# Output projection of a hybrid attention layer: eight block products of the matrix product, or seven with sums of blocks

## The chip, the cores and the metric

The kernel runs on one core of one Trainium2 chip. The metric is device time in microseconds (us), 958.43 as the median of three runs (957.11 to 959.27).

## The reference, cut to what matters

One encoder layer over 16 meta tokens and 512 real tokens of width 2048. After the two attention mixers, the gated outputs of all 16 heads are put side by side, projected once, normalised and added to the input:

```python
ya = gqa_axial_mixer(...) * jax.nn.silu(ga)            # 8 heads of 128
yb = diff_attn_mixer(...) * jax.nn.silu(gb)            # 8 heads of 128
y = jnp.einsum('blc,cd->bld', jnp.concatenate([ya, yb], axis=-1), w_out[layer])
h = h + rmsnorm(y, post_norm_g[layer])
return h[:, N_META:, :]
```

The change concerns the `einsum` with `w_out` alone: a product of 512 x 2048 (tokens by channels) with 2048 x 2048, and what follows it.

## The kernel before, in words

Every matrix product in single precision is made of three products of a split operand: an operand `a` becomes `ah` (rounded by ScalarE, helper `hi`) and `al = a - ah` (VectorE, helper `lo`), and `mm` is issued for high x high, low x high and high x low. For weights the same split is made by `wload`: a transfer of 512 KB into a tile `st`, then `wh` on ScalarE (L150) and `wl` on VectorE (L151). The tiles `st`, `wh` and `wl` have three buffers each, in the pool `wp`. `fetch` keeps a list of chunks: it loads and splits up to three chunks ahead of the one it gives out.

Work is dealt out by a planner, `Lanes`. The dense products are the main stream; the steps of each attention head are tasks that `lanes.poll()` slips in between matmuls when a modelled clock says that they are due. The order on TensorE is thereby fixed when the kernel is built, and so is the order on every other engine, where the scheduler of the framework has put the instructions by priority. Each engine takes its instructions strictly in that order, and one that waits holds up all behind it.

All loads and stores go through the queue of SyncE (SP). GpSimd (POOL) has a few small operations of each head: the scaling of the maximum `mxA`, the scaling of the probabilities `p`, the copy `pm`, and at the end the square root `ry`.

The last dense product with the input is the gate of head A7. Up to there both kernels are the same. Then the memory of the normalised input (`xh`, `xl`, pool `xp`) is given up for the pool `op`, which holds the channels of the heads as 16 pairs `oh`, `ol` of 128 x 512. Twelve of the 16 heads come back from scratch memory in six transfers `os` of 512 KB, which use `st` buffers too; the last four heads of mixer A are taken directly from `gA`, when they are ready.

`dense_out(g)` computes 512 output columns for all four token tiles: 16 channel tiles x 4 token tiles x 3 matmuls of 128x128 by 128x512, 192 in all, and there are four of them, 768 matmuls. Each chunk of weights has two channel tiles, so it feeds 24 matmuls. During the first of the four, the last attention heads are still interleaved. Results: `collect` makes the sum of squares (ScalarE, `jko`) and multiplies by the gain (VectorE, `y`), both straight from the accumulators; `finish` does the normalisation and the residual `xr`, and stores.

Of the kernel before, what the change touches and what calls it, by code (L numbers as in the profile page):

```python
# [10 lines left out]
F32 = mybir.dt.float32  # L11
# [97 lines left out]
def kernel(ctx: ExitStack, tc: tile.TileContext, xT, xn, xm, w_s, w_t, w_q, w_o,  # L109
# [8 lines left out]
    wp = ctx.enter_context(tc.tile_pool(name="wp", bufs=3))  # L118
    dr = ctx.enter_context(tc.tile_pool(name="dr", bufs=1, space=DRAM))
# [9 lines left out]
    oscr = [dr.tile([2, P, SEQ], F32, name=f"oscr{i}", tag=f"oscr{i}") for i in range(6)]  # L129

    def ctile(shape, name, dt=F32, src=None):
        t = cst.tile(shape, dt, name=name, tag=name)
        if src is not None:
            load(t, src)
        return t
# [6 lines left out]
    def wload(src, n=1024, dma=nc.sync.dma_start, parts=1):  # L142
        st = wp.tile([P, 1024], F32, name="st", tag="st")
        wh = wp.tile([P, 1024], F32R, name="wh", tag="wh")
        wl = wp.tile([P, 1024], F32R, name="wl", tag="wl")
        for i in range(parts):
            c = slice(i * n // parts, (i + 1) * n // parts)
            dma(out=st[:, c], in_=src if parts == 1 else src[:, c])
            with tc.high_priority(AHEAD):
                nc.scalar.activation(wh[:, c], st[:, c], AF.Copy)  # L150
                nc.vector.tensor_tensor(out=wl[:, c], in0=st[:, c], in1=wh[:, c].bitcast(F32),  # L151
                                        op=ALU.subtract)
# [29 lines left out]
    def fetch(ahead=2):  # L182
        while todo and len(chunks) <= ahead:
            chunks.append(wload(todo.pop(0)))
        return chunks.pop(0)
# [80 lines left out]
    cosT = ctile([P, TT, P], "cosT", src=cos_d)  # L266
    sinT = ctile([P, TT, P], "sinT", src=sin_d)
    gqB = ctile([P, P], "gqB", src=gq)
    gkB = ctile([P, P], "gkB", src=gk)
# [39 lines left out]
    def queries_B(pss):  # L309
# [5 lines left out]
        l1 = ap.tile([P, SEQ], F32R, name="l1", tag="ql", bufs=4)  # L315
        l2 = ap.tile([P, SEQ], F32R, name="l2", tag="ql", bufs=4)
# [188 lines left out]
    def attention_A(h, qn, q_task, k, k_task, v, v_task):  # L505
# [43 lines left out]
        over[NH + h] = last  # L549
        if h < 4:  # L550
            over[NH + h] = lanes.spawn(spill_A(h), 0.0, last)
# [70 lines left out]
    def queries_A(g):  # L622
# [13 lines left out]
        for t in range(TT):  # L636
            tag = "ql" if g == 0 else "fr" if t < 2 else "f"
            qn = ap.tile([P, 4, P], F32, name="qn", tag=tag, bufs=2 if tag == "fr" else 4)
# [25 lines left out]
    for grp in range(4):  # L664
        todo += [w_o[grp, :, k0:k0 + 2, :] for k0 in range(0, KT, 2)]
# [194 lines left out]
```

## Time and profile before

| | |
|---|---|
| median of three runs | 958.43 us |
| the profiled execution, its own time | 958.46 us |
| its span | 956.5 us |
| TensorE matmul busy | 934.7 us, 98% |
| weight loads of TensorE busy | 818.2 us, 86% |
| VectorE busy | 525.5 us, 55% |
| ScalarE busy | 457.9 us, 48% |
| GpSimd busy | 127.7 us, 13% |
| DMA queue of SP, share of the 16 DMA engines | 31.1% |
| the output projection | 751 to 948 us of the span |
| last matmul to the end of the span | 8.8 us |

A matmul is pipelined with the next, so its busy time of 395 ns is not what it costs; that is the distance of one from the next. Where the text names a time such as 762.09, it is counted from the start of the span of this execution. PE is TensorE, DVE VectorE, ACT ScalarE, POOL GpSimd, SP SyncE; PEclk is the granted clock of TensorE as a share of full speed.

### The profile page before, as it was taken

How to read it: one execution, taken by the hardware profiler on the slowest of the kernel's cores; microseconds unless marked ns; L12 is line 12 of the kernel's file. 1: busy time of each engine (PE TensorE's matmuls, PEld its weight loads, DVE VectorE, ACT ScalarE, POOL GpSimd, SP SyncE). 2: the span in 40 equal slices, each digit the busy share in tenths (PEclk: the TensorE clock that was granted, in tenths of full speed). 3: DMA queues.
4: the chain of work that ended last, by engine and by line, in shares of the span. 5: the costliest groups of instructions: out<-in, count | busy, mean ns of one | idle time of the engine just before them, and what ended most of it. 6: DMA issues, size and time to landing. Idle time of an engine off the chain costs nothing.

```text
span 956.5 us, 13979 instructions
## 1 busy us (share of the span) xinstructions
PE 934.7 (98%) x5530; PEld 818.2 (86%) x5530; DVE 525.5 (55%) x900; ACT 457.9 (48%) x812; POOL 127.7 (13%) x211
## 2 busy tenths in 40 slices
PE   7999999999999999999999999998999999999996
PEld 6889898989989898998998888886888888888884
DVE  6276675747575574756654274447554663232325
ACT  6665555547464553746552253354555742221221
POOL 0001010101001010100201041225212120000002
PEclk9999999999999999999999999998999999999999
DMA  9752222322223122222223223111222344623314
GB/s 318 252 180 77 85 90 68 97 77 94 82 73 104 66 99 77 86 82 68 91 75 94 94 66 110 57 66 56 77 77 67 114 128 158 238 88 98 101 45 175
DMA packets 31426, 99.31 MB, mean 104 GB/s; under 512 B 3681, under 2 KB 5601, under 8 KB 30721
## 3 DMA queue, kind: packets, MB, share of 16 engines
q1 hardware_dynamic: 31216, 98.42, 31.1%
q8 instruction: 43, 0.70, 0.3%
q14 instruction: 23, 0.18, 0.1%
q10 hardware_dynamic: 144, 0.01, 0.0%
HBM read 91.07 MB, written 7.34 MB: 103 GB/s over the span
## 4 chain that ended last, share of the span: by engine, by line
PE 89%; DVE 4%; ACT 2%; DMA 2%; POOL 2%; issue 1%; SPq 0%; DVEq 0%; POOLq 0%; ACTq 0%
PE pd L63 55%; PE po L63 19%; PE sc L63 6%; PE pv L63 5%; PE tr L66 5%; DMA xns<-in_xn_dram 2%; DVE qn L567 1%; DVE wl L151 1%; POOL ssh L228 1%; ACT qn L639 0%; ACT jk L564 0%; PE ss L63 0%; POOL qn L581 0%; ACT p L537 0%; DMA gcol<-in_gpre_dram 0%
## 5 line engine op out<-in xcount | busy, mean ns | idle before, releaser
L63 PE MATMUL pd<-xh,wh 128*128 128x264 f32 (+1 forms) x992 | 334.8, 337 | 4.9 <-ACT wh L150 4.9
L63 PE MATMUL pd<-xh,wl 128*128 128x264 f32 (+1 forms) x992 | 326.4, 329 | 0.3 <-DVE wl L151 0.3
L63 PE MATMUL pd<-xl,wh 128*128 128x264 f32 (+1 forms) x992 | 326.1, 329 | 0.0
L150 ACT ACTIVATE wh<-st 128x1024 fp32r<-128x1024 f32 (+2 forms) x139 | 144.4, 1039 | 278.0 <-PE po L63 95.8
L151 DVE TENSOR_TENSOR wl<-st,wh 128x1024 fp32r<-128x1024 f32 (+2 forms) x139 | 167.2, 1203 | 176.0 <-ACT wh L150 174.7
L63 PEld LDWEIGHTS pd<-xh,wh 128*128 128x128 f32 x992 | 188.4, 190 | 17.6 <-ACT wh L150 4.9
L63 PEld LDWEIGHTS pd<-xh,wl 128*128 128x128 f32 x992 | 187.7, 189 | 18.0 <-DVE wl L151 0.7
L63 PEld LDWEIGHTS pd<-xl,wh 128*128 128x128 f32 x992 | 188.6, 190 | 11.6
L63 PE MATMUL po<-wh,ol 128*128 128x512 f32 x256 | 101.0, 395 | 0.9 <-DVE ol L296 0.9
L63 PE MATMUL po<-wl,oh 128*128 128x512 f32 x256 | 101.9, 398 | 0.0
L63 PE MATMUL po<-wh,oh 128*128 128x512 f32 x256 | 101.7, 397 | 0.0
L450 ACT ACTIVATE p<-p,mx 128x528 f32<-128x528 f32 x64 | 46.5, 728 | 34.2 <-POOL mx L447 34.0
L63 PEld LDWEIGHTS po<-wh,ol 128*128 128x128 f32 x256 | 48.1, 188 | 12.2 <-DVE ol L296 1.2
L440 DVE CUSTOM_DVE_ANT_0 p<-sc,dist 128x528 f32<-128x528 f32 x64 | 44.9, 701 | 24.0 <-PE sc L63 23.5
L63 PEld LDWEIGHTS po<-wl,oh 128*128 128x128 f32 x256 | 48.1, 188 | 11.2
L63 PEld LDWEIGHTS po<-wh,oh 128*128 128x128 f32 x256 | 48.1, 188 | 10.2
L63 PE MATMUL pd<-wh,xh 128*128 128x512 f32 x128 | 52.2, 408 | 0.8 <-DVE vf L287 0.8
L293 ACT ACTIVATE ph<-tr 128x512 fp32r<-128x512 f32 x64 | 37.6, 591 | 31.2 <-PE tr L66 30.9
L296 DVE TENSOR_TENSOR pl<-tr,ph 128x512 fp32r<-128x512 f32 x64 | 43.4, 688 | 16.1 <-ACT ph L293 14.9
L66 PE MATMUL tr<-ident,p 128*128 128x128 f32 (+1 forms) x320 | 50.8, 273 | 0.8 <-DVE pl L296 0.8
L63 PE MATMUL pd<-wh,xl 128*128 128x512 f32 x128 | 50.6, 395 | 0.0
L63 PE MATMUL pd<-wl,xh 128*128 128x512 f32 x128 | 50.5, 395 | 0.0
(161 smaller groups left out, 1292.1 us busy)
## 6 DMA issues: line engine op xcount, KB each, us to landing
st<-in_w_t_dram SPq DMA_DIRECT2D x82, 512.0 KB, 3.6
st<-in_w_o_dram SPq DMA_DIRECT2D x32, 512.0 KB, 3.6
st<-in_w_q_dram SPq DMA_DIRECT2D x16, 512.0 KB, 3.6
xs<-in_xT_dram SPq DMA_DIRECT2D x16, 264.0 KB, 5.1
xns<-in_xn_dram SPq DMA_DIRECT2D x8, 512.0 KB, 6.3
xr<-in_xn_dram SPq DMA_DIRECT2D x4, 1024.0 KB, 10.2
os<-oscr SPq DMA_DIRECT2D x6, 512.0 KB, 3.6
out_dram<-y SPq DMA_DIRECT2D x6, 512.0 KB, 2.7
```

The lines of the kernel that those rows point to most:

```text
L63: self._add(self.nc.tensor.matmul(out, lhsT, rhs, start=start, stop=stop), us)
L66: self._add(self.nc.tensor.transpose(out, in_, ident), 0.109)
L150: nc.scalar.activation(wh[:, c], st[:, c], AF.Copy)
L151: nc.vector.tensor_tensor(out=wl[:, c], in0=st[:, c], in1=wh[:, c].bitcast(F32), op=ALU.subtract)
L228: nc.gpsimd.tensor_tensor(out=dst, in0=dst, in1=mhalf[:rows, :dst.shape[1]], op=ALU.pow)
L293: nc.scalar.activation(dst, src, AF.Copy)
L296: nc.vector.tensor_tensor(out=dst, in0=src, in1=h.bitcast(F32), op=ALU.subtract)
L440: nc.vector.tensor_tensor_reduce(out=two(p), in0=sc[:, :, :HALF], in1=two(dist[:, w0:w0 + NT]), scale=1.0, scalar=-3.0e38, op0=ALU.add, op ...
L450: nc.scalar.activation(p2[m], p2[m], AF.Exp, scale=0.125, bias=mx[:, m:m + 1], accum_out=sm[:, m:m + 1])
L567: nc.vector.scalar_tensor_tensor(out=raw[:, i, :], in0=raw[:, i, :], scalar=ss[:rows, i:i + 1], in1=g[:rows], op0=ALU.mult, op1=ALU.mult)
```

## The change: what it does

The tokens are cut into two halves (`lo_`, `hi_`, 256 each), the channels into two halves (the heads of mixer B, `oscr[0..3]`, and those of mixer A, `oscr[4..7]`), and the output columns, within each of two groups `n` of 1024, into two halves of 512 (`r`). A product of 2 x 2 blocks is then made of seven products in place of eight, in Winograd's form of Strassen's scheme. Each `product` is a quarter of the size in every group: 4 chunks x 2 token tiles x 2 channel tiles x 3 matmuls = 48, and there are 7 x 2 of them, 672 matmuls of the same shape as before. A chunk now feeds 12 matmuls.

The seven operands, in the order in which they are used: `b00` (B heads, low tokens), `t1` (B heads, high minus low), `t3` (A minus B, high tokens), `t2` (`t3` plus B low), `b11` (A heads, high), `b10` (A heads, low), `t4` (`t2` minus A low). The differences are made on VectorE (L775, L825, L828, L831), and each operand is split by `hi` and `lo` (L299, L302), 28 splits of 128x512 in place of 16. All four last heads of A are now stored in scratch memory as well, and all A and B heads are read back after the attention is done.

The weights of four of the seven products are sums of blocks of `w_out`. They are made by transfers that add to what is in memory (`wadd`), issued by GpSimd, on eight tiles `chain[n, i]` (`ch` in the listings): first block (1,0) plus (1,1) for `t1`; then a fresh load of (0,0) plus (1,0) for `t3`; plus (1,1) for `t2`; plus (0,1) for `b11`. That is 32 accumulating transfers of 512 KB. Plain loads of weights go from 32 to 40: 24 through `st`, 16 into `ch`. Splits of weight chunks go from 32 to 56. Combining the products takes 28 VectorE and 4 GpSimd operations of 128x512 and 8 copies on ScalarE, and 14 of the 16 multiplications by the gain move from VectorE to GpSimd (L856).

```diff
+    def wadd(t, src):
+        nc.gpsimd.dma_start(out=t, in_=src, accum_op=ALU.add)
+    def summed(n, *more, fresh=None):
+        def step(i):
+            ws = wsplit(chain[n, i])
+            if fresh:
+                nc.sync.dma_start(out=chain[n, i], in_=block(n, *fresh, i))
+            for rc in more:
+                wadd(chain[n, i], block(n, *rc, i))
+            return ws
+        return [lambda i=i: step(i) for i in range(4)]
+    for part in (lambda n: plain(n, 0, 0), lambda n: summed(n, (1, 0), fresh=(0, 0)),
+                 lambda n: summed(n, (1, 1)), lambda n: summed(n, (0, 1)), lambda n: summed(n),
+                 lambda n: plain(n, 0, 1), lambda n: plain(n, 1, 1)):
+        todo += part(0) + part(1)
...
-    oh = [op.tile([P, SEQ], F32R, name=f"oh{j}", tag=f"oh{j}") for j in range(KT)]
-    ol = [op.tile([P, SEQ], F32R, name=f"ol{j}", tag=f"ol{j}") for j in range(KT)]
-    for j in range(0, KT - 4, 2):
-        st = wp.tile([P, 1024], F32, name="os", tag="st")
...
+    b00, t1 = [], []
+    for i in range(4):
+        st = heads_of(i, wp, "st")
+        b00.append(operand(op, "u", i, st[:, :, lo_]))
+        raw = op.tile([P, 2, NP], F32, name="t1r", tag="t1r")
+        nc.vector.tensor_tensor(out=raw, in0=st[:, :, hi_], in1=st[:, :, lo_], op=ALU.subtract)
+        t1.append(operand(op, "v", i, raw))
+    for n in range(2):
+        for i in range(4):
+            nc.sync.dma_start(out=chain[n, i], in_=block(n, 1, 0, i))
+            wadd(chain[n, i], block(n, 1, 1, i))
+    def product(ops, pool, tail=0, done=None):
+        pss = [pool.tile([P, 512], F32, name="po", tag="pd") for _ in range(2)]
+        def step(u, i, ws):
+            (bh, bl), (wh, wl) = ops[i], ws
+            tq = slice(u * P, (u + 1) * P)
+            for j in range(2):
+                c = slice(j * 512, (j + 1) * 512)
+                mm(pss[u], bh[:, j, tq], wh[:, c], start=(i + j == 0), stop=False)
+                mm(pss[u], bl[:, j, tq], wh[:, c], start=False, stop=False)
+                mm(pss[u], bh[:, j, tq], wl[:, c], start=False, stop=(i + j == 4))
+                lanes.poll()
...
+    t3, b11, b10, t2, sA = [], [], [], [], []
+    for i in range(4):
+        sB = heads_of(i, yp, f"y{i // 2}{i % 2}")
+        a = heads_of(4 + i, yp, f"sA{i}")
+        nc.vector.tensor_tensor(out=sB[:, :, hi_], in0=a[:, :, hi_], in1=sB[:, :, hi_],
+                                op=ALU.subtract)
+        t3.append(operand(yp, "w", i, sB[:, :, hi_]))
+        nc.vector.tensor_tensor(out=sB[:, :, lo_], in0=sB[:, :, hi_], in1=sB[:, :, lo_], op=ALU.add)
+        t2.append(operand(op, "u", i, sB[:, :, lo_]))
+        b11.append(operand(yp, "x", i, a[:, :, hi_]))
+        nc.vector.tensor_tensor(out=a[:, :, hi_], in0=sB[:, :, lo_], in1=a[:, :, lo_],
+                                op=ALU.subtract)
+        b10.append(operand(op, "v", i, a[:, :, lo_]))
...
+    def block_done(t, n, r, tt=TTp):
+        v = y[t, n][:, r * 512:(r + 1) * 512]
+        jk = yp.tile([P, 512], F32, name="jko", tag="jko")
+        nc.scalar.activation(jk, v, AF.Square, accum_out=ssy[t][:, 2 * n + r:2 * n + r + 1])
+        g = 2 * n + r
+        tt(out=v, in0=v, in1=gpB[:, g * 512:(g + 1) * 512], op=ALU.mult)
...
+    for n in range(2):
+        for u, ps in enumerate(product(b11, pd2)):
+            v = y[2 + u, n][:, G0]
+            TTv(out=v, in0=ps, in1=v, op=ALU.subtract)
+            block_done(2 + u, n, 0)
+    for t in (0, 1):
+        xr[t] = residual(t, "x")
+    for t in (2, 3):
+        partial(t, 3)
+        row_done(t, xr[t])
...
```

Three places of the order show what moves. The first is SP's queue at the start of the projection. `st` is a weight chunk, `os` a pair of heads read back, `ch` a tile of the chain. Before:

```order
L148 DMA st_7541<-in_w_o_dram 128x1024
L718 DMA os_7667<-oscr0_78 128x2x512
L718 DMA os_7673<-oscr1_79 128x2x512
L718 DMA os_7679<-oscr2_80 128x2x512
L718 DMA os_7685<-oscr3_81 128x2x512
L718 DMA os_7691<-oscr4_82 128x2x512
L718 DMA os_7697<-oscr5_83 128x2x512
L148 DMA st_7707<-in_w_o_dram 128x1024
```

The last row is the third weight chunk of the projection; it stands behind six reads of heads. In the changed kernel, from the same place:

```order
L767 DMA os_7673<-oscr2_83 128x2x512
L779 DMA ch00_7641<-in_w_o_dram 128x1024
L779 DMA ch01_7642<-in_w_o_dram 128x1024
L767 DMA os_7685<-oscr3_84 128x2x512
L779 DMA ch02_7643<-in_w_o_dram 128x1024
L779 DMA ch03_7644<-in_w_o_dram 128x1024
L779 DMA ch10_7645<-in_w_o_dram 128x1024
L779 DMA ch11_7646<-in_w_o_dram 128x1024
L779 DMA ch12_7647<-in_w_o_dram 128x1024
L779 DMA ch13_7648<-in_w_o_dram 128x1024
L148 DMA st_7715<-in_w_o_dram 128x1024
```

The third chunk (last row) now stands behind the fourth read of heads and six loads of the chain, and TensorE asks for it after 24 matmuls where it was 48. On GpSimd, at the same time, the accumulating transfers lie between the small operations of the last heads:

```order
L406 TENSOR_SCALAR pm_7572<-pm_7572 32x256
L684 DMA ch00_7641<-in_w_o_dram 128x1024
L540 TENSOR_SCALAR mxA_7626<-mxA_7626 128x1
L684 DMA ch01_7642<-in_w_o_dram 128x1024
L546 TENSOR_SCALAR p_7733<-p_7733,smA_7627 128x528
L684 DMA ch02_7643<-in_w_o_dram 128x1024
L684 DMA ch03_7644<-in_w_o_dram 128x1024
L540 TENSOR_SCALAR mxA_7787<-mxA_7787 128x1
L684 DMA ch10_7645<-in_w_o_dram 128x1024
```

Before, the four computing rows followed one another with nothing between; now each is behind accumulates that wait for the load of their tile. The third place is VectorE where `t3` starts, the beginning of the operand work for the last five products (`wl0`, `xl0`, `vl0`, `ul0` are low halves of the operands of `t3`, `b11`, `b10`, `t2` for the first chunk; `wl` without a digit is a weight chunk):

```order
L156 TENSOR_TENSOR wl_8227<-ch01_7642,wh_8226 128x1024
L825 TENSOR_TENSOR os_8252<-os_8254,os_8252 128x2x256
L156 TENSOR_TENSOR wl_8365<-ch02_7643,wh_8364 128x1024
L302 TENSOR_TENSOR wl0_8258<-os_8252,wh0_8257 128x512
L828 TENSOR_TENSOR os_8252<-os_8252 128x2x256
L302 TENSOR_TENSOR xl0_8267<-os_8254,xh0_8266 128x512
L302 TENSOR_TENSOR vl0_8272<-os_8254,vh0_8271 128x512
L302 TENSOR_TENSOR ul0_8263<-os_8252,uh0_8262 128x512
L831 TENSOR_TENSOR os_8254<-os_8252,os_8254 128x2x256
L825 TENSOR_TENSOR os_8275<-os_8277,os_8275 128x2x256
L302 TENSOR_TENSOR xl1_8290<-os_8277,xh1_8289 128x512
```

The same seven rows follow for chunks 1, 2 and 3, and only behind all 28 of them stands the split of the fourth weight chunk of `t3` (`wl<-ch03`). Before, there was nothing of the kind at that place: the projection was already running, and VectorE had one split per 24 matmuls and the multiplications by the gain.

More of the change, by code (lines that the diff above doesn't have):

```diff
@@ L183, in fetch @@
         while todo and len(chunks) <= ahead:
[L184 removed]
+            src = todo.pop(0)
+            chunks.append(src() if callable(src) else wload(src))
         return chunks.pop(0)
@@ L723, in dense_out @@
[L723 to L748 removed]
+    NP = TT // 2 * P
```

207 lines of the change are left out of this document (123 added, 84 removed).

## Prediction

> **What bounds the kernel now.** I read the page first (shares of engines, the chain that ended last), then the stretch of the output projection by windows, then the chain in order of time.
>
> ```profile
> PE 934.7 (98%) x5530; PEld 818.2 (86%) x5530; DVE 525.5 (55%) x900; ACT 457.9 (48%) x812; POOL 127.7 (13%) x211
> PE 89%; DVE 4%; ACT 2%; DMA 2%; POOL 2%; issue 1%; SPq 0%; DVEq 0%; POOLq 0%; ACTq 0%
> ...
> 803.50:947.50 144.00, 144.00 (x618) 115.63 (x616) 47.08 (x54) 34.63 (x54) 2.48 (x6) 1.00 0.38 128
> ...
> 762.09 1.40 PE po L63 x6
> 777.05 2.79 PE po L63 x12
> 803.34 0.12 PE pv L63
> 803.46 144.23 PE po L63 x618
> 947.78 0.70 ACT jko L770 x2
> 948.56 0.27 POOL ry L776
> 948.91 0.56 POOL ry L778
> 949.50 0.48 DVE y L788
> 950.78 1.80 DVE y L788
> ```
>
> TensorE bounds it. In the window row the first figure pair is TensorE: 144.00 of 144.00 us busy, at clock 1.00, while VectorE has 47 and ScalarE 35, and the DMA engines are at 0.38. The chain says the same: after the last attention matmul (pv, 803.34) it is one unbroken piece of projection matmuls, then a tail of ScalarE, GpSimd and VectorE. Twelve matmuls take 2.79 us, so one costs 0.2325 us. The profiled execution took 958.46 us (span 956.5), 0.03 from the median of the runs; the sum is made against 958.46.
>
> **What the change removes.** 768 matmuls become 672 of the same shape: 96 x 0.2325 = 22.3 us. With TensorE busy throughout, all of it is gained if TensorE stays busy: 936.2. The rest of this part is about where it doesn't.
>
> **Weight splits, 32 to 56.**
>
> ```profile
> L150 ACT ACTIVATE wh<-st 128x1024 fp32r<-128x1024 f32 x30 | 31.7, 1058 | 96.5 <-PE po L63 95.8 <-DMA st<-in_w_o_dram 0.7
> L151 DVE TENSOR_TENSOR wl<-st,wh 128x1024 fp32r<-128x1024 f32 x30 | 37.2, 1239 | 90.6 <-ACT wh L150 90.3 <-PE tr L66 0.3
> L296 DVE TENSOR_TENSOR ol<-os,oh 128x512 fp32r<-128x512 f32 x12 | 7.6, 684 | 1.1 <-ACT oh L293 1.0
> 754.77 3.09 DVE L296 TENSOR_TENSOR ol<-os,oh 128x512 fp32r<-128x512 f32 x5
> ```
>
> A chunk now lasts 2.79 us instead of 5.58, and its split takes 1.06 on ScalarE and 1.24 on VectorE. The 95.8 us that the splits waited for TensorE to free a buffer show the slack. In steady state I cost them at nothing; the cover is the 2.79 us of matmul, and it is gone wherever other VectorE work stands ahead of a split. An operand operation of 128x512 takes 0.684 us alone and 3.09 / 5 = 0.62 in a run.
>
> **First stall: the third weight chunk.** It is asked for after 24 projection matmuls, and the 25th starts the piece of the chain at 762.09. Its load stands behind one read of heads and six chain loads in SP's queue.
>
> ```profile
> st<-in_w_o_dram SPq DMA_DIRECT2D x32, 512.0 KB, 3.6
> 10.00:20.00 10.00, 10.00 (x56) 8.80 (x55) 8.98 (x12) 7.25 (x11) 0.00 (x0) 1.00 1.04 398
> 744.22 0.36 SPq L718 DMA_DIRECT2D os<-oscr  x1
> 751.85 0.68 DVE L296 TENSOR_TENSOR ol<-os,oh 128x512 fp32r<-128x512 f32 x1
> 752.57 0.42 DVE L296 TENSOR_TENSOR pm<-tr,pm 32x256 fp32r<-32x256 f32 x1
> 752.05 0.75 POOL L400 TENSOR_SCALAR pm<-pm 32x256 fp32r<-32x256 f32 x1 [1.61 <-ACT pm L293]
> 755.01 0.49 POOL L534 TENSOR_SCALAR mxA<-mxA 128x1 f32<-128x1 f32 x1 [2.22 <-DVE mxA L533]
> ```
>
> A single 512 KB load lands 3.6 us after issue; with the DMA engines saturated (share 1.04) they move 398 GB/s, so 524,288 bytes cost 1.32 us. The third read of heads goes out at 744.22, and two chain loads with it, early enough. The fourth needs the buffer of the first, which VectorE gives up after its low half (the place of the row at 751.85), `pm` (752.57 to 752.99) and the new difference `t1r` (0.68): 753.7. From there, 3.6 for it and 7 x 1.32 = 9.2 for the six chain loads and the chunk: it lands at 766.5. Split on both engines, 1.06 + 1.24, it is ready at 768.8; the third matmul, the first to use the low half, was due at 762.56. Floor of the stall: 6.2 us.
>
> On top come the accumulating transfers, which this trace does not have. Their engine time C is at least that of a load, 1.32, and at most a load plus a store, 2.64, since a tile is also read. A gain is excluded: they are extra bytes on the same engines. Two are out before: GpSimd is free after `pm` at 752.8, and after `mxA` at 755.5. Those delay the chunk by 2C. From the third on each waits for its chain tile, about 761; during the remaining six transfers of SP's queue (7.9 us) they take at most an equal share. At C = 1.32 some three get in, 4.0: stall 6.2 + 2.6 + 4.0 = 12.8. At C = 2.64 it is 6.2 + 5.3 + 7.9 = 19.4. I take 12.8, from the nearest row, which is also the middle of 6.2 and 19.4. The small GpSimd operations of the heads wait 2 to 4 us behind accumulates there, but what needs them on TensorE is itself behind the stall. The later `pm` at 787.88 can be late by 0 to 1 us; I leave it out.
>
> The Trainium skill, page "Collectives: The Full Stack", section "The bandwidth ceiling: the fold count and why AG ≠ RS ≠ AR", says that a reduce in the DMA engines runs at half the rate of a copy because it reads two sources. By that rule C would be 2.64 and the first stall 19.4, the sum 969; no run here shows it yet.
>
> **Second stall: operands at the start of `t3`.** From the last matmul of `t1`, which frees a weight buffer, VectorE must wait for `wh<-ch02` (1.06), do two weight splits (2 x 1.24) and 27 of the 28 operand operations before TensorE has the low half of the fourth chunk: 27 x 0.62 = 16.7 to 27 x 0.684 = 18.5, together 20.2 to 22.0 us. TensorE has three chunks and two matmuls to do meanwhile, 3 x 2.79 + 0.47 = 8.8. Stall 11.4 to 13.2; I take 12.3. Reading back the heads (stored at the end of attention, 42 matmuls or 9.8 us ahead of `t3`) takes a store and a load of 3.6 and then one pair per 2.6 us, while VectorE eats a pair in 4.5 us, so it is hidden behind VectorE.
>
> **Third stall: behind `b11`.** VectorE's normalisation of tokens 256 to 511 stands ahead of the fourth split of `b10` and waits for GpSimd.
>
> ```profile
> L581 POOL TENSOR_TENSOR qn<-qn,cosT x8: 1292/1335/2212, 560.2 to 668.4; 128x512 f32<-128x512 f32 x8
> L776 POOL TENSOR_SCALAR ry<-ssy,ssp 128x1 f32<-128x1 f32 x4 | 1.1, 267 | 147.2 <-ACT jko L770 147.2
> L778 POOL TENSOR_TENSOR ry<-ry,mhalf 128x1 f32<-128x1 f32 x4 | 2.2, 557 | 0.3
> L788 DVE SCALAR_TENSOR_TENSOR y<-y,ry,xr 128x1024 f32<-128x1024 f32 x6 | 7.4, 1280 | 1.0 <-POOL ry L778 1.0
> L771 DVE TENSOR_TENSOR y<-po,gpB 128x512 f32<-128x512 f32 x16 | 11.0, 691 | 11.7 <-ACT jko L770 11.5
> L770 ACT ACTIVATE jko<-po 128x512 f32<-128x512 f32 x16 | 9.6, 599 | 22.2 <-PE po L63 22.0
> ```
>
> After its last matmul: combine 0.69, square 0.80 (0.60 and the read of the sum), GpSimd's multiplication 1.34, two `ry` 0.53, one power 0.56: 3.9. Eight halves of the 1024 form, 0.64 each: 9.0; the split: 10.3. TensorE can go on for 8.8. Stall 1.5, between 0 and 3.
>
> **The tail** is a subtraction more and 0.5 us less of the last VectorE pieces: I leave it at 8.8. The other combining operations have 22 us per pair of products beside 9.9 us of splits and cost nothing; the 32 accumulates cost 8C = 10.6 to 21.1 per 22.3 us and are hidden too.
>
> Sum: 958.46 - 22.3 + 12.8 + 12.3 + 1.5 = 962.8, so 963.
>
> **Rivals.**
> (a) *Faster.* The first stall decides. If accumulates reach the DMA engines late, because GpSimd takes long to issue one, the chunk lands near 766.5 and the stall is 6.2 to 7.5; with the low ends of the other two (11.4, 0.5) the sum is 954.3 to 955.6. It decides from a sum of stalls under 20.4 us. For it: GpSimd takes 0.49 us for one element per partition (the row at 755.01), and making up a transfer is more than that. Against it: the floors alone are 6.2 + 11.4.
> (b) *Accumulates at a load plus a store*: 969, as above. For it: a tile must be read as well. Against: read and write sides may overlap.
> (c) *Accumulates become the bound.* If C is above 2.8, eight no longer fit into 22.3 us. At twice a load plus a store, 5.3, `t2` and `b11` would each be 8 x 5.3 - 22.3 = 20 us late: about 1000. No row speaks for it.
> (d) *The clock.* TensorE idles for 12 us in the first stall.
>
> ```profile
> 940.00:956.50 16.50, 7.68 (x33) 5.83 (x32) 10.12 (x10) 2.11 (x6) 4.07 (x7) 0.89 0.57 229
> ```
>
> In the last 16.5 us the clock row falls to 0.89 when TensorE is idle for 8.8. If half speed lasted for a few us after a stall, that is 1 to 2 us more, 964 to 965, inside the range. The Trainium skill, page "TensorE: Matmul & The Clock Gate", section "What's actually happening", has half clock after an idle window of about 3.4 us and as long again to recover; that is an estimate of 1.7 us per long stall, and the row above is all that this trace shows of it.
>
> **How the numbers follow.** Likeliest, with (d), 0.48: 963, own range 957 to 967. (b) 0.24, (a) 0.18, (c) 0.10. What a measurement of this kernel can tell from no change is about 0.2%, 1.9 us. Faster than 956.5 is (a) and the edge of the likeliest, 0.19; between 956.5 and 960.3 lies the lower part of the likeliest, 0.13; the rest, 0.68, is slower. The range leaves out (c) and half of the low end of (a): 953 to 978.
>
> **What would show it.** Matmuls of `po` 672 in place of 768, each 0.2325 apart. A gap on TensorE of 6 to 19 us near 762, ended by ScalarE's `wh` or its DMA; accumulates on a queue of their own, 16.8 MB. Near 820, three gaps that add up to 11 to 13 us, ended by VectorE's L302 and L156. A gap of up to 3 us ended by L156 some 9 us after `b11`. It is wrong if TensorE has no gap at the third chunk, if VectorE's operand operations are much shorter than 0.62, or if TensorE waits for accumulates in `t2` and `b11`.

## The result, and the profile after

The seven products took 1003.72 us (median of four runs, 1002.95 to 1004.26), the eight 958.41 beside them: a ratio of 1.0473, 95% interval 1.0455 to 1.0491. The forecast was 963, between 953 and 978. The direction was right; the size was not. The profiled execution has a span of 1002.3 us against 956.5, so 45.8 us are to be found, and 22.3 more, since the saved matmuls are really gone.

The rows of the page after: engines, the two DMA queues (packets, MB, share of the 16 engines' span), the chain by engine.

```profile
PE 925.4 (92%) x5434; PEld 806.1 (80%) x5434; DVE 590.6 (59%) x972; ACT 493.9 (49%) x856; POOL 183.6 (18%) x261
q1 hardware_dynamic: 36304, 106.81, 32.2%
q0 software_dynamic: 4608, 16.78, 8.7%
PE 76%; DMA 8%; DVE 7%; ACT 3%; POOL 3%; issue 2%; SPq 0%; DVEq 0%; POOLq 0%; ACTq 0%
```

5434 matmuls are 96 fewer than 5530. TensorE's share of the chain fell from 89% to 76%, and transfers and VectorE took it over. Queue q0 holds the 32 accumulating transfers and nothing else: 8.7% of 1002.3 us over 32 is 2.73 us of all 16 DMA engines for each.

The stretch of the projection by windows (TensorE's busy time, weight loads, VectorE, ScalarE, GpSimd, the granted clock, the DMA engines' share, GB/s):

```profile
762.20:787.00 24.80, 5.02 (x13) 3.40 (x14) 5.96 (x9) 4.21 (x7) 6.24 (x8) 0.59 1.05 291
833.00:876.00 43.00, 20.12 (x60) 14.02 (x59) 22.70 (x33) 15.25 (x23) 5.39 (x7) 0.71 0.79 227
904.00:925.00 21.00, 16.86 (x69) 13.06 (x68) 21.00 (x17) 10.24 (x18) 14.14 (x10) 0.95 0.69 147
945.00:960.00 15.00, 11.69 (x44) 9.03 (x43) 10.69 (x14) 4.90 (x8) 4.46 (x7) 0.89 0.79 288
986.50:1002.30 15.80, 4.12 (x18) 3.00 (x16) 8.44 (x11) 2.17 (x5) 4.29 (x5) 0.75 0.34 133
```

Where before there was one window of 144.00 busy of 144.00, there are now five places with holes. In the first the DMA engines are full (share 1.05), and in the second they were up to 852 (1.06 from 828 to 852); in the third VectorE is busy for all of its 21.00 us.

**The account.** For each stretch I take its length less the matmuls in it at their pace (0.2325 us for one of the projection). This holds the gaps and the slow matmuls behind them. From 751.4 to the end of `t1` (837.3): 28.0 lost, against 3.3 before in the same work, so 24.7, of which 22.5 lie between 761.4 and 787.0. From there to 890, the start of `t3`: 30.4. From 890 to the last matmul: 11.2 against 0.6, that is 5.4 at `b11`, 5.1 at `b10` and little else. The tail after the last matmul is 11.7 against 8.8: 2.9. Together 24.7 + 30.4 + 10.6 + 2.9 = 68.6, and 68.6 - 22.3 = 46.3, against 45.8 measured.

**First stall.** TensorE's rows (the idle time ahead of an instruction and its releaser in brackets), then the issue of the load that ends it and the split that waited for that load:

```profile
781.94 0.80 PE L63 MATMUL po<-wh,uh 128*128 128x512 f32 x1 [19.76 <-ACT wh L155]
784.22 0.63 PE L63 MATMUL po<-wh,ul 128*128 128x512 f32 x1
784.65 0.63 PE L63 MATMUL po<-wl,uh 128*128 128x512 f32 x1
786.57 0.39 PE L63 MATMUL po<-wh,uh 128*128 128x512 f32 x1
786.80 0.40 PE L63 MATMUL po<-wh,ul 128*128 128x512 f32 x1
```
```profile
758.16 4.07 SPq L148 DMA_DIRECT2D st<-in_w_o_dram  x2
780.83 1.06 ACT L155 ACTIVATE wh<-st 128x1024 fp32r<-128x1024 f32 x1 [12.14 <-DMA st<-in_w_o_dram]
```

A gap of 19.76 us ahead of the third chunk. Its load went out at 758.16 and was there when ScalarE split it at 780.83, 22.7 us later, where a load of that size took 3.6 before. After the gap two matmuls start 0.43 apart (784.22, 784.65), four rows on 0.23 apart (786.57, 786.80): the clock stood at half speed for some 4 us.

**Second stall**, the start of `t3`: the time to landing of the eight reads of heads issued between 828 and 852, VectorE's rows and TensorE's.

```profile
DMA to landing us min/median/max: 10.0/22.6/26.6
```
```profile
848.83 0.69 DVE L825 TENSOR_TENSOR os<-os 128x512 f32<-128x512 f32 x1 [11.87 <-DMA os<-oscr]
859.45 0.69 DVE L825 TENSOR_TENSOR os<-os 128x512 f32<-128x512 f32 x1 [5.18 <-DMA os<-oscr]
850.24 0.79 PE L63 MATMUL po<-wh,wh 128*128 128x512 f32 x1 [12.60 <-ACT wh L299]
862.05 0.79 PE L63 MATMUL po<-wh,wh 128*128 128x512 f32 x1 [6.44 <-ACT wh L299]
872.33 0.50 PE L63 MATMUL po<-wh,wh 128*128 128x512 f32 x1 [1.49 <-ACT wh L299]
875.40 0.79 PE L63 MATMUL po<-wl,wh 128*128 128x512 f32 x1 [1.84 <-DVE wl L156]
```

VectorE itself waited 11.87 and 5.18 us for the heads that are read back; their reads took 10.0 to 26.6 us. The first two gaps on TensorE follow from these waits, the last two from VectorE's and ScalarE's own work.

**`b11`, `b10` and the tail.** VectorE's and GpSimd's rows and TensorE's two gaps, in order of time:

```profile
904.13 3.83 POOL L902 TENSOR_TENSOR y<-y,y 128x512 f32<-128x512 f32 x2 [2.18 <-DVE y L901]
904.50 4.55 DVE L156 TENSOR_TENSOR wl<-ch,wh 128x1024 fp32r<-128x1024 f32 x2
907.92 2.29 POOL L856 TENSOR_TENSOR y<-y,gpB 128x512 f32<-128x512 f32 x1
910.68 2.79 DVE L156 TENSOR_TENSOR wl<-ch,wh 128x1024 fp32r<-128x1024 f32 x1
910.78 1.60 POOL L856 TENSOR_TENSOR y<-y,gpB 128x512 f32<-128x512 f32 x1
918.12 0.68 DVE L900 TENSOR_TENSOR y<-po,Q 128x512 f32<-128x512 f32 x1
918.29 1.28 POOL L902 TENSOR_TENSOR y<-y,y 128x512 f32<-128x512 f32 x1 [5.06 <-DVE y L901]
918.72 1.40 DVE L302 TENSOR_TENSOR ul<-os,uh 128x512 fp32r<-128x512 f32 x1
920.65 4.50 DVE L156 TENSOR_TENSOR wl<-ch,wh 128x1024 fp32r<-128x1024 f32 x2
921.81 2.25 POOL L902 TENSOR_TENSOR y<-y,y 128x512 f32<-128x512 f32 x1
922.98 0.80 PE L63 MATMUL po<-wl,xh 128*128 128x512 f32 x1 [3.74 <-DVE wl L156]
942.24 2.98 POOL L856 TENSOR_TENSOR y<-y,gpB 128x512 f32<-128x512 f32 x2 [7.90 <-ACT jko L854]
946.29 5.39 DVE L884 SCALAR_TENSOR_TENSOR y<-y,ry,xr 128x512 f32<-128x512 f32 x8 [2.98 <-POOL ry L875]
952.87 0.50 PE L63 MATMUL po<-wl,vh 128*128 128x512 f32 x1 [3.31 <-DVE wl L156]
```

A weight split, 1.24 us before, takes 4.55 / 2 = 2.3, 2.79 and 4.50 / 2 = 2.25 us while GpSimd works on tiles. The first of the two at 920.65 is the one that TensorE waits for: the third chunk of `b11` comes 3.74 us late. At `b10` the normalisation of tokens 256 to 511 (eight pieces, 5.39 us) stands ahead of the split and waits for GpSimd, which first makes two multiplications by the gain. In the tail VectorE's pieces for tokens 0 to 127 stand ahead of the last combination, which begins 1.5 us after the last matmul is done:

```profile
989.49 2.74 DVE L884 SCALAR_TENSOR_TENSOR y<-y,ry,xr 128x512 f32<-128x512 f32 x4 [0.80 <-POOL ry L875]
990.22 0.40 PE L63 MATMUL po<-wl,uh 128*128 128x512 f32 x1
992.14 0.68 DVE L922 TENSOR_TENSOR y<-y,po 128x512 f32<-128x512 f32 x1
```

### The profile page after: what moved, and what is told of

It is laid out like the page before. It is cut to its first block, busy times and chain, and to the rows that moved or that the text cites. A ratio compares the mean times of both kernels' runs of the same rounds, so it can differ in the third digit from the quotient of the medians.

```text
span 1002.3 us, 14093 instructions
## 1 busy us (share of the span) xinstructions
PE 925.4 (92%) x5434; PEld 806.1 (80%) x5434; DVE 590.6 (59%) x972; ACT 493.9 (49%) x856; POOL 183.6 (18%) x261
## 4 chain that ended last, share of the span: by engine, by line
PE 76%; DMA 8%; DVE 7%; ACT 3%; POOL 3%; issue 2%; SPq 0%; DVEq 0%; POOLq 0%; ACTq 0%
PE pd L63 51%; PE po L63 11%; PE sc L63 5%; PE pv L63 4%; PE tr L66 4%; DMA os<-oscr 3%; DMA st<-in_w_o_dram 2%; DVE wl L156 2%; DMA xns<-in_xn_dram 2%; DMA ch<-in_w_o_dram 1%; DVE qn L571 1%; DVE y L884 1%; POOL qn L585 1%; ACT wh L155 1%; POOL ssh L234 1%
## 5 line engine op out<-in xcount | busy, mean ns | idle before, releaser
L155 ACT ACTIVATE wh<-st 128x1024 fp32r<-128x1024 f32 (+2 forms) x131 | 135.9, 1038 | 221.5 <-PE pd L63 92.5
L156 DVE TENSOR_TENSOR wl<-st,wh 128x1024 fp32r<-128x1024 f32 (+2 forms) x131 | 158.4, 1211 | 119.3 <-ACT wh L155 118.3
L156 DVE TENSOR_TENSOR wl<-ch,wh 128x1024 fp32r<-128x1024 f32 x32 | 45.9, 1442 | 22.8 <-ACT wh L155 22.5
L63 PE MATMUL po<-wh,uh 128*128 128x512 f32 x96 | 39.4, 411 | 20.3 <-ACT wh L155 19.8
L155 ACT ACTIVATE wh<-ch 128x1024 fp32r<-128x1024 f32 x32 | 33.8, 1057 | 46.1 <-PE po L63 40.6
L302 DVE TENSOR_TENSOR pl<-tr,ph 128x512 fp32r<-128x512 f32 x64 | 43.4, 688 | 16.1 <-ACT ph L299 14.9
L299 ACT ACTIVATE ph<-tr 128x512 fp32r<-128x512 f32 x64 | 37.6, 591 | 30.5 <-PE tr L66 30.4
L66 PEld LDWEIGHTS tr<-ident,p 128*128 128x128 f32 (+1 forms) x320 | 37.3, 132 | 14.6 <-DVE gA L551 2.7
L453 POOL TENSOR_SCALAR mx<-mx 128x2 f32<-128x2 f32 x32 | 12.1, 377 | 195.9 <-DVE mx L446 195.9
L543 ACT ACTIVATE p<-sc,mxA 128x528 f32<-128x528 f32 x32 | 22.4, 700 | 48.3 <-POOL mxA L540 48.1
```

The lines of the kernel that those rows point to most:

```text
L63: self._add(self.nc.tensor.matmul(out, lhsT, rhs, start=start, stop=stop), us)
L66: self._add(self.nc.tensor.transpose(out, in_, ident), 0.109)
L299: nc.scalar.activation(dst, src, AF.Copy)
L302: nc.vector.tensor_tensor(out=dst, in0=src, in1=h.bitcast(F32), op=ALU.subtract)
L453: nc.gpsimd.tensor_scalar(out=mx, in0=mx, scalar1=-0.125, scalar2=1.0, op0=ALU.mult, op1=ALU.mult)
L543: nc.scalar.activation(two(p), sc[:, :, :HALF], AF.Exp, scale=ASCALE, bias=mx, accum_out=sm)
```

## Experiments

Times are medians; the ratio to the kernel before, with its interval, stands behind each. The runs come from several chips, on which the kernel before took 956.6 to 958.6 us in the median, so a difference of 1 to 2 us between two of them can be the chip's; the ratio is against the same chip. Theory A is the engine time of the accumulates, C VectorE's operand operations, D the clock, G VectorE beside GpSimd.

**`no_sums` and `plain_loads`: what an accumulate costs.**

```diff
-        nc.gpsimd.dma_start(out=t, in_=src, accum_op=ALU.add)
+        pass                                        # no_sums
+        nc.gpsimd.dma_start(out=t, in_=src)         # plain_loads
```

> The changed kernel without its 32 accumulating transfers: the sums of weight blocks are left out, every load stays where it was. Theory A (the DMA engines: an accumulate takes 2.73 us of all 16, a load 1.3, and in two bursts the loads that TensorE needs stand among accumulates): the first stall falls from 19.8 us to 6 to 8, the gaps at the start of t3 from 22.4 to 11 to 14 (VectorE's 27 operand operations), the one before 922.98 goes, and less time is spent at a low clock: 965 to 976 in place of 1003.7. Theory B (the order in SP's queue: the third chunk behind six chain loads, the heads behind seven fresh loads; accumulates are beside the point): both stalls keep over two thirds, 990 or more.

> The 32 accumulating transfers become plain loads into the same tiles, on the same queue of GpSimd, with the same waits: the sums are left out, the bytes from HBM are the same. If the cost of an accumulate is that of reading and writing its tile (theory A): GpSimd's queue falls from 8.7% of the engines' time to 4 to 5%, the first stall from 19.8 to 11 to 14, and the time is 978 to 992, about half way to the kernel without them. If what costs is a second queue beside SP's, GpSimd's issue or the waits between transfers: within 5 us of 1003.7.

Measured: 971.33 without them (1.0147, 1.0117 to 1.0177), 983.29 with plain loads (1.0272, 1.0242 to 1.0302). The first gap of `no_sums` and of `plain_loads`, and the queue of the latter:

```profile
767.05 0.80 PE L63 MATMUL po<-wh,uh 128*128 128x512 f32 x1 [7.07 <-ACT wh L155]
```
```profile
776.14 0.80 PE L63 MATMUL po<-wh,uh 128*128 128x512 f32 x1 [13.45 <-ACT wh L155]
q0 software_dynamic: 4608, 16.78, 4.8%
```

In `no_sums` the time to landing of the eight reads of heads, and the matmul that first uses the low half of the fourth chunk of `t3`:

```profile
DMA to landing us min/median/max: 5.3/8.2/9.6
840.73 0.79 PE L63 MATMUL po<-wl,wh 128*128 128x512 f32 x1 [1.83 <-DVE wl L156]
```

Same bytes from HBM, same queue, same waits, and 4.8% of 981.9 us over 32 is 1.47 us each in place of 2.73. The first gap is 7.07, 13.45 and 19.76 us for none, loads and accumulates; the time lost at the start of `t3` is 14.5, 19.6 and 30.4, and the eight reads land 8.2, 14.6 and 22.6 us after issue in the median. Theory A holds, and theory B, SP's order alone, falls. The accumulates are worth 32 us of the 45: 12 for 32 more transfers, 20 for the adding. One expectation was missed: the gaps at `t3` without them sum to 7.2 us and not 11 to 14. The rest of the 14.5 is matmuls that run slowly between and behind them. From the last matmul of `t1` to the row at 840.73 it is 21.3 us, of which 12.5 are lost.

**`before_accum`: the same cost where nothing waits.**

```diff
             ws = fetch()
+            if g:
+                nc.gpsimd.dma_start(out=scr[j0 // 2 % 5], in_=w_o[g, :, j0:j0 + 2, :],
+                                    accum_op=ALU.add)
```

> The kernel before (eight products) with 21 accumulating transfers of 512 KB added in the last three quarters of its projection, into tiles that nobody reads. If 2.73 us of all engines is what an accumulate costs by itself: GpSimd's queue at 6.0% of the engines' time, and since the engines are otherwise 0.25 to 0.38 busy there, the time is within 1.5 us of before. If the 2.73 came of contention with loads: 3 to 4% and no change. If accumulates also slow down the work of engines on the same memory: 3 us or more slower.

Measured: 957.88 against 958.55 (0.9994, 0.9983 to 1.0005). Its queue and the DMA row in 40 slices:

```profile
q0 software_dynamic: 3024, 11.01, 5.8%
DMA  8752222322223122221223223111222344999514
```

5.8% of 957.4 us over 21 is 2.64 us. The engines are full here too (the slices with 9), so this share alone doesn't separate the transfer's own price from contention. The packets in the trace do: one of 4,096 bytes of an accumulate takes 327 to 328 ns at the median, with packets of another queue in flight or with none, and 128 of them over 16 engines make 2.62 us; in `plain_loads` such a packet of the same queue takes 159 ns. And though the engines are full, nothing is lost, since a chunk lasts twice as long and is loaded well ahead. So an accumulate does no harm by itself; it does where a load that TensorE needs is issued late and stands among several.

**`late_chain`: the burst moved off the third chunk.**

```diff
-    for n in range(2):
-        for i in range(4):
-            nc.sync.dma_start(out=chain[n, i], in_=block(n, 1, 0, i))
-            wadd(chain[n, i], block(n, 1, 1, i))
+            ws = wload(block(n, 0, 0, i))
+            for j in ((2 * i - 4, 2 * i - 3) if n == 0 else (i + 4,)) if n or i > 1 else ():
+                t = chain[j // 4, j % 4]
+                nc.sync.dma_start(out=t, in_=block(j // 4, 1, 0, j % 4))
+                wadd(t, block(j // 4, 1, 1, j % 4))
```

> The changed kernel with one change of order: the eight first loads of the chain tiles and their accumulates are issued behind the chunks of b00 from the third chunk on, in pairs and then singly, in place of ahead of the third chunk. Engine time is the same. Theory A (a burst stands ahead of the third chunk; spread over b00's 50 us the work fits: 14 transfers of 1.3 and 8 of 2.73 are 40 us): the stall of 19.8 us shrinks to under 2, and with the slow matmuls behind it 19 to 22 us are gained: 981 to 986. Rival (the burst only moves on: t1 then waits for its chain tiles): a new gap of 8 us or more at the start of t1, 990 or more.

Measured: 992.2 (1.0355, 1.0318 to 1.0392). That is the rival's number, but not for the rival's reason.

```profile
766.41 0.79 PE L63 MATMUL po<-wh,uh 128*128 128x512 f32 x1 [4.96 <-ACT wh L155]
836.60 0.80 PE L63 MATMUL po<-wh,wh 128*128 128x512 f32 x1 [13.03 <-ACT wh L299]
```

The gap fell to 4.96, not under 2: the scheduler orders by readiness, and three of the chain's loads and two accumulates (issued at 752.1 and 754.9) still went ahead of the third chunk, whose load went out at 756.1 and took 9 us. `t1` never waited for its tiles, as theory A had it. But the start of `t3` lost 31.9 us, 1.5 more than before the edit: the first burst and the second are separate, and each has to be taken away by itself.

**`lazy`: VectorE's part at `t3`.** Only `t3`'s operands are made ahead of it.

```diff
-        t2.append(operand(op, "u", i, sB[:, :, lo_]))
-        b11.append(operand(yp, "x", i, a[:, :, hi_]))
-        b10.append(operand(op, "v", i, a[:, :, lo_]))
+        for u, ps in enumerate(product(t3, pd2, hook=(for_t2, for_b11)[n])):
+        for u, ps in enumerate(product(t2, pd, hook=(for_b10, None)[n])):
```

> The changed kernel with only t3's operands made ahead of t3 (12 operations, 8 of them on VectorE); those of t2 and b11 are made behind each chunk of t3, those of b10 behind those of t2. Theory C (VectorE's 27 operations set the end of the second stall): 9 to 11 us less, 993 to 995. Theory A (the heads' read back sets it, landing 18 to 26 us after issue): the wait for the first two pairs stays, the rest shortens, 3 to 7 us less, 997 to 1001.

Measured: 994.9 (1.0393, 1.0346 to 1.0441), C's number, though the interval, 990 to 999 us, reaches into A's. The first two gaps stay:

```profile
849.29 0.80 PE L63 MATMUL po<-wh,wh 128*128 128x512 f32 x1 [12.06 <-ACT wh L299]
859.97 0.79 PE L63 MATMUL po<-wh,wh 128*128 128x512 f32 x1 [5.28 <-ACT wh L299]
```

Both theories are right in part: the time lost at `t3` goes from 30.4 to 23.0, and 17.3 of what is left are these two gaps, the wait for the heads.

**`no_gpsimd`: the gap at `b11`.**

```diff
-            TTp(out=c11, in0=u3, in1=c11, op=ALU.add)
-            block_done(2 + u, n, 1)
+            block_done(2 + u, n, 1, None)     # without the multiplication by gpB
```

> The changed kernel without GpSimd's eight operations in t2 (four additions and four multiplications by the gain are left out). Theory G (VectorE's operations take up to twice as long while GpSimd works on tiles: weight splits of 2.3 and 2.8 us in place of 1.2): the splits in t2 and b11 stay at 1.2 to 1.3 us, the gap of 3.7 us at b11 goes with the slow matmuls behind it, 997 to 999. If VectorE has simply too many operations there (21 us busy of 21): the gap stays over 2 us, 1001 to 1004.

Measured: 997.34 (1.0404, 1.0373 to 1.0435), 6.4 us less than the changed kernel. The split that took 2.3 us:

```profile
905.68 1.22 DVE L156 TENSOR_TENSOR wl<-ch,wh 128x1024 fp32r<-128x1024 f32 x1
```

No gap is left at `b11`. VectorE's operations were not too many; they were slowed. In the rows of the changed kernel the operation that reads PSUM (`y<-po,Q` at 918.12, 0.68) is not slowed beside GpSimd's addition at 918.29, in this one row; the next one, with both inputs in SBUF (`ul<-os,uh`), takes 1.40 in place of 0.68. That agrees with the Trainium skill, page "SBUF — State Buffer", section "Who interferes with whom": an instruction of VectorE with both inputs in SBUF contends with a GpSimd instruction that reads SBUF.

**`filled` and `filled2`: the clock.** Matmuls of no use fill the gaps.

```diff
+            if fill:
+                idle(pool, fill)      # filled: 75; 45, 22.  filled2: 91; 58, 22, 22
             for u in range(2):
                 step(u, i, ws)
```

> The changed kernel with 142 more matmuls of no use (75 ahead of the third chunk of b00, 45 and 22 ahead of the first two chunks of t3, into a bank that nobody reads), which fit into gaps of 19.8, 12.6 and 6.4 us. Theory D (TensorE's clock falls while it idles and the matmuls after a gap run slowly; such matmuls sum to 10.2 us more than 0.2325 each in the changed kernel, some 6 of them behind these three gaps): the clock stays at 1.0 there and the time is 996 to 999. If the low clock costs nothing, or only follows from waiting for data: 1002 to 1006.

> As filled, with 193 matmuls of no use: 91 ahead of the third chunk of b00, and 58, 22 and 22 ahead of the first, second and fourth chunk of t3, so that gaps under 1 us are left there (filled left 3.8, 3.2 and 6.0 us, and the clock fell behind them all the same). Theory D (a gap of over 3 us costs 2.3 to 2.6 us more behind it, 12 or 13 matmuls at 0.43 in place of 0.2325): the slow matmuls' sum falls from 10.2 us to 3 to 5 (b11's and b10's gaps are left) and the time to 996 to 1000. If the time behind a gap is set by what VectorE and ScalarE deliver: the sum falls and the time stays, 1001 to 1005.

Measured: 1003.52 (1.0484, 1.043 to 1.0537) and 1009.42 (1.054, 1.0511 to 1.0568). The first left gaps over 3 us and told little. In the second, one fill stood beside the gap it was meant for:

```profile
870.47 0.80 PE L63 MATMUL po<-wl,wh 128*128 128x512 f32 x1 [6.06 <-DVE wl L156]
874.90 5.60 PE L63 MATMUL junk<-uh 128*128 128x512 f32 x22
```

These 22 cost some 5.4 us for nothing. Without them it would be about 1004, an estimate: no gain, though the clock stayed at 1.00 through the first stall and the slow matmuls summed to 6.8 us in place of 10.2. Where the clock was kept up, the next wait took the time (3.76 us for `pm` behind the first stall). So theory D is not shown as a cause; each is a pair of runs, with intervals of 5 and 3 us to each side, and a smaller gain would not show.

**`early`, `early_lazy`, `paced`: the sums made during the attention.** 32 copies and 32 accumulates into DRAM, and 56 plain loads in the projection.

```diff
+        if stage == 0:
+            nc.gpsimd.dma_start(out=dst, in_=first)
+        else:
+            nc.gpsimd.dma_start(out=dst, in_=block(n, r, c, i), accum_op=ALU.add)
...
+            if calls[0] > 6 and jobs:          # in dense_T, behind each fetch
+                presum(*jobs.pop(0))
```

`paced` wraps both transfers in `tc.keep_in_program_order`.

> The four sums of weight blocks are made in DRAM during the attention (32 copies and 32 accumulates of 512 KB on GpSimd's queue, one transfer behind each fetch of weights there), and the projection then loads 56 plain chunks. Theory A (what costs is the engine time of the accumulates inside the projection): no stall at the third chunk, at t3's start VectorE's 12 us and 2.6 at a low clock, the gaps at b11 and b10 (3.7 and 3.3, each with some 2.6 at a low clock) and the 2.9 us longer tail stay: 962 to 970. Rival (64 transfers, some 170 us of engine time, and their issue on GpSimd disturb the attention, where the engines are 0.2 to 0.3 busy): 975 or more.

> As early, with the operands of t2, b11 and b10 made behind the chunks of t3 and t2. Theory C for what is left at t3 (VectorE's 27 operations): 6 to 11 us less than early, 953 to 961. If the reading back of the heads sets it also without accumulates: at most 3 less than early.

> As early, but each of the 64 transfers keeps its place in GpSimd's stream behind the attention's own GpSimd operations, so that they spread over the attention in place of its first 200 us. In early the stretch from the first projection matmul to the end took 216.0 us (after 250.4, before 204.5). If the burst alone disturbed the attention: that stretch stays within 3 us of 216 and the first projection matmul comes at 752 to 758, 966 to 973. If 170 us of engine time disturb the attention wherever they lie: 980 or more.

Measured: 1062.7 (1.1091, 1.1049 to 1.1132), 1061.26 (1.1076, 1.1028 to 1.1123) and 967.13 (1.0089, 1.0064 to 1.0114). The DMA rows of `early` and of `paced`:

```profile
DMA  9998999822312222122222222311122265774762
```
```profile
DMA  9743466675557457555663263121122558574862
```

In `early` GpSimd, which has little to do there, ran ahead and put out all 64 transfers in the first 200 us, where TensorE starved for weights (busy for 129 of the 200 us, 193 before). Held behind GpSimd's own operations they spread, and the attention lost nothing: the first matmul of the projection comes at 749.8, where it came at 845.7 in `early` and at 751.2 before. `early_lazy` gained 1.4, not 6 to 11: the scheduler had put nearly all operand operations ahead of the split of the fourth chunk again, so the run does not test C.

**`paced_lazy`, `best`, `best_gain`, `best_tail`, `spread`: what is left.** Each builds on the one before it, `spread` on `best_gain`.

```diff
+        keep(nc.scalar.activation(h, src, AF.Copy))          # paced_lazy: operands pinned in order
+        keep(nc.vector.tensor_tensor(out=l, in0=src, in1=h.bitcast(F32), op=ALU.subtract))
+        for u, ps in enumerate(product(b10, pd, hook=(rows, None)[n])):    # best
-    nc.sync.dma_start(out=gpB, in_=gpost)          # best_gain: issued behind t3's products
+        row_done(u, xr[u], True)                   # best_tail, in end(u, ps)
-        for u, ps in enumerate(product(b11, pd2, hook=(for_b10, for_t4)[n])):
+        for u, ps in enumerate(product(b11, pd2,   # spread
+                                       hook=(None, lambda i: (for_b10(i), for_t4(i)))[n])):
```

> As paced, with the operands made where the program says (each pinned behind what its engine was given before): t3's ahead of t3, t2's behind the chunks of its first half, b11's behind those of its second, b10's and t4's during b11. Theory C (VectorE's operand operations are what is left at t3 and, with t4's four, at b11): the gaps at t3 fall from 9 to 10 us to 2 to 4, that at b11 from 3.7 to under 2, 8 to 13 less than paced. If VectorE is short of time in t3 and t2 as a whole, the gaps come back in t2: at most 4 less.

> As paced_lazy, with the normalisation of tokens 256 to 511 behind the second and third chunk of b10 instead of ahead of its fourth split, and that of tokens 0 to 127 behind the last combination instead of ahead of it. The gap at b10 (3.3 to 5.5 us, 2.6 more at a low clock) goes and the tail of 11.7 us is 1 to 2 shorter: 6 to 9 less than paced_lazy, 945 to 953, faster than before by 0.6 to 1.4%. If GpSimd is late with its share wherever that stands: within 2 us of paced_lazy.

> As best, with the 1 MB load of the gain vector issued behind t3 in place of ahead of t3's fourth chunk. If SP's order and those bytes made the fourth chunk late (its load went out at 816.5 behind eight reads of heads and this one): the gap of 5.0 us before it at t3 falls to 1 to 3, and with it the slow matmuls behind: 2 to 6 less, 954 to 958. If the chunk waits for a free buffer or ScalarE: within 1 us of best's 960.1.

> As best_gain, with the tail back in the order of the changed kernel (tokens 0 to 127 normalised ahead of the last combination), but a quarter of them on ScalarE and GpSimd as it was done for the last tokens alone. In best the tail took 13.1 us from the last matmul, 5.8 of it VectorE's seven pieces in a row. Here two pieces less stand on VectorE behind the last combination or ahead of it: 10 to 11 us, 2 to 3 less than best_gain, 951 to 955. If GpSimd's additions become the end: no gain over best_gain.

> As best_gain, with VectorE's work spread: the operands of b10 beside t4's in the second half of b11 (none while GpSimd works on the tiles of t2), two pieces of the normalisation of tokens 256 to 511 behind each of four chunks of b10 in place of four behind each of two, and in the tail the three pieces of tokens 0 to 127 between the last combination and its multiplication by the gain, where VectorE waits for ScalarE. Theory C (VectorE ahead of a weight split is what is left): the gaps at b11 (0.9, 0.9, 0.5) and b10 (1.7, 1.9) go to under 0.5 each and the tail of 13.1 us becomes 10 to 11: 950 to 954, faster than before by 0.4 to 0.8%. If the gaps come from GpSimd's share of the combinations or from the chunks' loads, they stay and the time is within 2 us of best_gain's 957.9.

Measured: `paced_lazy` 964.87 (1.0068, 1.0046 to 1.009), only 2.3 less than `paced`: the gaps came back elsewhere, though at `b10` (6.9 us) and not in `t2`. `best` 960.08 (1.0017, 1.0005 to 1.0028), not the 945 to 953 expected: the gap at `b10` became two of 1.7 and 1.9, but the tail stayed at 13.2 us. It had been 13.2 in `paced` and `paced_lazy` already; the expectation took 11.7 from the changed kernel. In `paced` the 1.5 us between them lie behind the last computing operation, and their cause is open. `best_gain` 957.88 (1.0002, 0.9993 to 1.0012), 2.2 less on another chip, with an interval that overlaps that of `best`: the largest gap at `t3` in `best`, then the same place in `best_gain`:

```profile
829.46 0.79 PE L63 MATMUL po<-wh,wh 128*128 128x512 f32 x1 [4.96 <-ACT wh L155]
```
```profile
824.59 0.50 PE L63 MATMUL po<-wh,wh 128*128 128x512 f32 x1 [1.66 <-ACT wh L155]
```

A 1 MB load that was issued at 815.1 and first used at 867.1 had stood ahead of that chunk in SP's queue; it is the third chunk of `t3`, not the fourth as expected. `best_tail` 957.4 (0.9995, 0.9984 to 1.0006), no gain over `best_gain`: its tail was 13.5, not 10 to 11; the last combination waited for VectorE's three pieces of the tokens ahead. `spread` 954.28 (0.9963, 0.995 to 0.9975) is the one version that beats both kernels, by 0.4%. Its last two gaps at `b10`:

```profile
906.22 0.50 PE L63 MATMUL po<-wl,vh 128*128 128x512 f32 x1 [0.41 <-DVE wl L156]
916.87 0.50 PE L63 MATMUL po<-wl,vh 128*128 128x512 f32 x1 [1.45 <-DVE wl L156]
```

The forecast of under 0.5 held for one of the two, and the tail came to 12.0, not 10 to 11. By the account it still loses 5.9 us at `t3`, 8.0 behind it and 3.2 in the tail: most of the 22.3 saved.

## Why the prediction was wrong, and where it was right

1. *96 matmuls, -22.3.* Right: 5434 records, and 0.23 apart where nothing is short.
2. *First stall, 12.8.* The place and the mechanism were right: the fourth read of heads was forecast for 753.7 and went out at 753.83, and `no_sums` showed a gap of 7.07 where the floor was put at 6.2. The step that failed is the engine time C of an accumulate: taken at 1.32, "the nearest row", it is 2.73. With 2.64 the same steps gave 19.4, and 19.76 was measured. With plain loads, that is with nearly the C that I took (1.47), the gap was 13.45 against 12.8. Rival (b) had it. The rule of the Trainium skill that it cited, page "Collectives: The Full Stack", section "The bandwidth ceiling: the fold count and why AG ≠ RS ≠ AR", that a reduce runs at half the rate of a copy, is said there of collectives; this case agrees with it, with 2.73 and 2.64 against 1.47 for the plain load on the same queue. But (b) carried the price only into this stall and gave 969, which would still have been inside the range.
3. *Second stall, 12.3.* The largest miss, 30.4. The step that failed: "Reading back the heads ... takes a store and a load of 3.6 and then one pair per 2.6 us ... so it is hidden behind VectorE". Those eight reads stand behind the fresh chain loads and share the engines with accumulates, which took 65% of the engines' time between 828 and 852. They took 22.6 us in the median and 26.6 at most, and VectorE waited 17 us for them. In `no_sums` they took 8.2 and 9.6, and VectorE waited 1 us. VectorE's own term was well sized: there the low half of the fourth chunk was used 21.3 us after the last matmul of `t1`, 20.2 to 22.0 forecast, and 12.5 us were lost up to it, 12.3 forecast. With rival (b)'s 969, the 18 us missed here are what takes the sum out of the range.
4. *Third stall, 1.5.* Place and cause right (`b10`'s fourth split behind the normalisation); the gap was 3.31, over the upper bound of 3, and 5.1 with the slow matmuls. The term that was too small is GpSimd's: one multiplication of 1.34 was counted, and two in a row take 2.98 (942.24) ahead of `ry`. No run took this wait away by itself; `best` cut it from the 6.9 of `paced_lazy` to 1.7 and 1.9.
5. *"The other combining operations ... cost nothing."* Wrong by 5.4 at `b11`. The sum of VectorE's times had room, but at durations measured without GpSimd beside it; `no_gpsimd` took the gap away.
6. *The tail, unchanged.* 11.7 in place of 8.8. The forecast counted the operations behind the last matmul and not those of the tokens ahead, which hold VectorE when the last combination is due (the rows of the tail above). That is 1.5 of the 2.9; the rest is the subtraction and a longer `ry` on GpSimd.
7. *The clock, rival (d), 1 to 2 us.* As a mechanism right, as a size too small: slow matmuls sum to 10.2 us against 1.0 before, because there were five long stalls and not one: 2 us for each, where the prediction's estimate was 1.7. As a cost of its own it is not shown; at `t3` without accumulates the slow matmuls fell inside VectorE's time. The Trainium skill, page "TensorE: Matmul & The Clock Gate", section "What's actually happening", names an idle window of about 3.4 us; here the gaps of 3.3 us and more in the changed kernel were followed by 4 to 11 matmuls 0.43 apart. Of the gaps under 2 us some were followed by none (1.66 in `best_gain`) and some by as many (1.83 in `no_sums`, 3 us behind another gap, by 10), so the length of a single gap did not decide it.
8. *Rival (c), accumulates as the bound.* Not seen: eight of 2.73 are 21.8 of the 22.3 us of a pair of products, and the DMA engines came close to full, yet no gap in `t2` or `b11` waits for a chain tile.

The range failed because the two cases that I treated as rivals to each other, a dearer accumulate and a late load, are one: once C doubles, every load issued inside a burst is late, in the second stall as in the first.

## What to carry to other kernels

Price a new kind of transfer by both of its bounds at every place where a load that is needed soon can stand behind it, not only at the place where it is first met; then look for bursts, since full DMA engines cost nothing where loads run well ahead. Work that is hidden by a sum of times must be hidden in its order as well: what stands ahead of each weight split on VectorE, and which engine reads the same memory then. A saving of 22 us on the bounding engine was used up here by five waits, and only when the sums, the operands, the normalisation and the gain vector's load had all been moved did 3 us of it come through.

## What the runs showed of the hardware

- An accumulating transfer of 512 KB into SBUF takes 2.73 us of all 16 DMA engines (2.64 in `before_accum`), a plain load on the same queue 1.47; their packets of 4,096 bytes take 327 and 159 ns at the median. Its issue takes GpSimd 0.91 us in the mean of the 32.
- VectorE's split of 128x1024 takes 1.22 us alone and 2.25 to 2.8 beside GpSimd's additions and multiplications of tiles.
- 64 transfers of GpSimd that were not held in its program order went out in the first 200 us of `early` and lengthened the part ahead of the projection by some 94 us; held in its order, in `paced`, they lengthened it by nothing.
- Full DMA engines cost nothing by themselves: in `before_accum` their share is 1.06 from 820 to 880, and TensorE is busy for all of the 60 us.
